# A two-layer attention and feed-forward trunk on one core: low parts of weight blocks moved from GpSimd to VectorE in the seven-product stage, and two tile pairs held instead of three

## Chip, cores and metric

One core of a Trainium2 chip runs the kernel. The metric is device time in microseconds, the median of several runs. The engines are named as the profile names them: PE (TensorE; PEld is its weight load), DVE (VectorE), ACT (ScalarE), POOL (GpSimd) and SP (SyncE, which here only issues DMAs).

## What is computed

Two transformer layers over 1024 latent tokens and 256 context tokens, width 1024. Layer 0 has windowed attention with grouped keys, layer 1 neighbourhood attention. Each layer ends with a gated feed-forward part, and that part is what the change touches:

```python
def swiglu(h, w_gu, w_down):
    gu = h @ w_gu
    return (jax.nn.silu(gu[..., :D_FF]) * gu[..., D_FF:]) @ w_down
...
        h = h + gt1 * y
        h = h + gt2 * swiglu(modulate(h, g_ffn[i], sh2, sc2), w_gate_up[i], w_down[i])
```

D_FF is 2816, which is 22 tiles of 128. Everything is float32.

## The kernel before

**Precision.** A float32 operand is split into a high part, rounded to the type that PE takes (fp32r), and a low part, the rest. A product is then three matmuls: high by high, high by low, low by high. `split` (L139) does this for a 128x512 block: ACT casts the high part (L141), and the engine given as `lo` subtracts it for the low part (L142).

**The stage.** `back` (L805) is the second half of a layer: output projection (`wo`, L860), normalisation, gate-up product, down product (L1061). In the gate-up product the contraction is cut into two halves of 512 and the 1024 tokens into two halves, and gate and up stand as the two block rows of a 2x2 block matrix a11, a12, a21, a22 (`load_gu`, L947: `raw` for gate blocks, `rawf` for up blocks, three buffers each). So a *tile pair* f (gate tile f and up tile f, f from 0 to 21) is a 2x2 by 2x2 block product, done with seven block products instead of eight. Each of them (`product`, L796) is 4 x 3 = 12 matmuls of 128x512, all recorded at L802. The token side is B11, B21, T1 to T4 and B22, made once per layer (`norm_lat`, `combine`). The weight side of a pair is a11, a12 and five sums (`weights`, L972): s1, s2, s3, a22 itself and a last s2. They are made on DVE by the helper `add` (L1159) into tiles `wt` and split into tiles `px`.

**Order of a pair.** `first` (L957) does the products with B11 and B21; ACT copies the first to u2 (L961) and puts the Silu of the sum into sg (L964). `second` (L967) adds the product with T2 to u2. `third` (L985) does T3 and T1 into two banks, which DVE reads as u3 (two additions); then it goes on filling the same two banks with T4 and B22, so those wait for u3. Of the results, s0 and y1 go to DRAM (L995, L1000). u2, sg and u3 are tiles `kp`, from eight buffers (`keep`, L818).

**What sets the order of the work.** The products with B11 and B21 of the first NPRE = 6 pairs are done ahead, while the other token blocks are made: their a11 and a12 are split into `wsp` tiles (`ew`, L1003 to L1006). Of these six pairs the u2 and sg of the first HELD = 3 stay in SBUF. Those of the rest are spilled to DRAM (L1019) and loaded back in the main loop (L1033). The instructions are put in order per engine by a scheduler when the program is built, so an edit of one place can move others. Each engine, and SP's DMA queue, then works strictly in its order.

Of the kernel before, what the change touches and what calls it, by code (L numbers as in the profile page):

```python
# [52 lines left out]
class Trunk:  # L53
# [751 lines left out]
    def back(self, layer, o):  # L805
# [8 lines left out]
        xslot = lambda dt=F32R: px.tile([P, 2, 512], dt, name="px", tag="px")  # L814
# [59 lines left out]
        def norm_lat(c):  # L874
            rs = self.rstd(st[c])
            if c == 0:
                self.preload(AF.Silu, rs[:, :1])
            yield
            pb = self.rows(rs, 4)
            yield  # L880
            g, sh = self.gsc[layer][1], mod[:, 3]
            for j in range(4):
                for k in (j, j + 4):
                    t, b = h[c, k], sh[:, k, 0:1]
                    nc.vector.scalar_tensor_tensor(out=t, in0=t, scalar=g[:, k, 0:1], in1=pb, op0=ALU.mult, op1=ALU.mult)
                    if c == 0:
                        nc.scalar.activation(out=t, in_=t, func=AF.Identity, bias=b)
                        B["B11" if k < 4 else "B21", j] = self.split(t, self.pslot(), alt(k + k // 4))
                        yield
            if c == 0:  # L890
                return
            for j in range(4):

                nc.vector.scalar_tensor_tensor(out=h[0, j], in0=h[1, j], scalar=sh[:, j, 0:1], in1=h[0, j],
                                               op0=ALU.add, op1=ALU.subtract)
                t2 = tmp()
                nc.vector.scalar_tensor_tensor(out=t2, in0=h[1, j + 4], scalar=sh[:, j + 4, 0:1], in1=h[0, j],
                                               op0=ALU.add, op1=ALU.subtract)
                B["t2", j] = t2
                B["T2", j] = self.split(t2, self.pslot(), "vector")  # L900
                for k in (j, j + 4):
                    nc.scalar.activation(out=h[1, k], in_=h[1, k], func=AF.Identity, bias=sh[:, k, 0:1])
                yield
# [43 lines left out]
        def load_gu(f, which):  # L947
            r = []
            for i, (y, half) in enumerate(which):
                t = (self.raw, rawf)[y]()  # L950
                nc.sync.dma_start(out=t, in_=a[f"w_gu{layer}"][f, y][:, half * 512:half * 512 + 512])
                r.append(t)
            return r
# [15 lines left out]
            self.product(pb, S, tb("T2"), True, True)  # L969
            self.add(u2, pb, u2, ALU.add)  # L970

        def weights(f, slot=xslot):  # L972

            a11, a12, a21, a22 = load_gu(f, ((0, 0), (0, 1), (1, 0), (1, 1)))
            if f >= NPRE:
                yield self.split(a11, xslot(), "gpsimd"), self.split(a12, xslot(), "gpsimd")
            s1 = self.add(wt(), a21, a22, ALU.add)
            s2 = sub(s1, a11)
            yield self.split(s2, xslot(), "gpsimd")
            s3 = sub(a11, a21)  # L980
            rest = [self.split(x, xslot(), "gpsimd") for x in (s3, s1, a22)]
            self.add(s2, a12, s2, ALU.subtract)
            yield rest + [self.split(s2, xslot(), "gpsimd")]

        def third(f, u2, sg, S):  # L985
            pd = self.bank()
# [12 lines left out]
            self.add(y1, y1, u3, ALU.mult)  # L999
            nc.sync.dma_start(out=self.ss[layer][f, :, 512:1024], in_=y1)  # L1000

        NPRE, HELD = 6, 3
        ew = []  # L1003
        for f in range(NPRE):
            a11, a12 = load_gu(f, ((0, 0), (0, 1)))
            ew.append([self.split(a11, self.slot(), "gpsimd"), self.split(a12, self.slot(), "vector")])  # L1006
        g1 = norm_lat(1)
        next(g1)
        if not last:
# [14 lines left out]
        for f in range(NF):  # L1024
            w = weights(f)
            if f >= NPRE:
                u = first(f, next(w))
            elif f < HELD:
                u = U[f]
            else:  # L1030
                u = keep(), keep()
                for i in range(2):
                    nc.sync.dma_start(out=u[i], in_=self.us[layer][f, i])  # L1033
            second(u[0], next(w))
            third(f, *u, next(w))
# [239 lines left out]
```

## Time and profile before

| what | value |
|---|---|
| median of 3 runs | 2933.78 us (2933.45 to 2938.89) |
| the profiled execution | 2932.86 us |
| its span | 2931.0 us |
| mean granted PE clock | 0.991 |
| PE busy | 97% |
| PEld busy | 79% |
| DVE busy | 54% |
| ACT busy | 38% |
| POOL busy | 37% |

The profile is one execution. Its span runs from the first to the last instruction, so it is 1.86 us shorter than that execution's time. Busy shares are averages over stages with different limits; a busy PE may still run at a lower clock.

### The profile page before, as it was taken

Reading aid. Unit: us, or ns where it says so; the run is one execution under the profiler, and the core shown is the slowest. Engines: PE = TensorE matmul, PEld = TensorE weight load, DVE = VectorE, ACT = ScalarE, POOL = GpSimd, SP = SyncE. Lnnn points to the kernel's source line nnn. Section 1 sums busy time; section 2 is a strip of 40 time slices with the busy share of each in tenths; the row PEclk is TensorE's granted clock in tenths of the full one; section 3 lists DMA queues with packets and bytes.
Section 4 is the critical chain, followed back from the end, with each engine's and each line's share of the span. In section 5 each row is a group of like instructions: output and inputs, shape, how many; then the busy total and the mean of one; then the engine's idle time right before and its main releaser. Section 6 shows DMA issues by size and latency. Waiting matters only on the chain.

```text
span 2931.0 us, 42778 instructions
## 1 busy us (share of the span) xinstructions
PE 2845.3 (97%) x15586; PEld 2305.4 (79%) x15586; DVE 1596.1 (54%) x2765; ACT 1124.5 (38%) x2263; POOL 1080.0 (37%) x1002
## 2 busy tenths in 40 slices
PE   6999999998999999999999999999999899999999
PEld 3667777787888887778998888777788788887887
DVE  5667777547655545446543344265656745555442
ACT  4323676434223232234543223265644422333120
POOL 3453242114555442233872345011102555554220
PEclk8999999999999999999999999999999999999999
DMA  7573342532322248544652554356653322226221
GB/s 265 189 232 94 101 126 80 165 110 100 129 83 80 81 165 287 193 159 136 191 184 88 151 153 139 99 159 162 179 171 124 125 93 82 87 83 205 87 90 61
DMA packets 305026, 402.09 MB, mean 137 GB/s; under 512 B 30000, under 2 KB 165680, under 8 KB 304816
## 3 DMA queue, kind: packets, MB, share of 16 engines
q1 hardware_dynamic: 235920, 360.81, 38.7%
q10 hardware_dynamic: 68896, 38.55, 4.5%
q8 instruction: 123, 2.02, 0.3%
q14 instruction: 87, 0.71, 0.1%
HBM read 316.69 MB, written 82.58 MB: 136 GB/s over the span
## 4 chain that ended last, share of the span: by engine, by line
PE 86%; DVE 4%; DMA 4%; ACT 2%; POOL 2%; issue 1%; SPq 1%; DVEq 0%; POOLq 0%; ACTq 0%
PE b L802 16%; PE bm L1061 16%; PE bm L802 10%; PE bm L352 10%; PE bm L860 7%; PE bm L1122 4%; PE b L352 3%; PE b L598 3%; PE b L588 3%; PE b L740 2%; PE b L1061 2%; PE b L725 2%; DMA qst<-q_s 2%; PE b L555 1%; PE b L159 1%
## 5 line engine op out<-in xcount | busy, mean ns | idle before, releaser
L1061 PE MATMUL bm<-pr,wsp 128*128 128x512 f32 x1920 | 440.3, 390 | 0.0
L1061 PEld LDWEIGHTS bm<-pr,wsp 128*128 128x128 f32 x1920 | 359.2, 188 | 82.1 <-issue 6.7
L802 PE MATMUL b<-wsp,px 128*128 128x512 f32 x1584 | 382.0, 395 | 11.0 <-DVE kp L1159 11.0
L802 PEld LDWEIGHTS b<-wsp,px 128*128 128x128 f32 x1584 | 300.9, 190 | 78.1 <-DVE kp L1159 11.9
L142 POOL TENSOR_TENSOR px<-wt,px 128x512 fp32r<-128x512 f32 x176 | 237.1, 1360 | 246.9 <-ACT px L141 238.9
L842 DVE SCALAR_TENSOR_TENSOR px<-bm,mod,px 128x512 f32<-128x512 f32 (+1 forms) x232 | 170.7, 739 | 279.8 <-PE bm L1061 223.5
L802 PE MATMUL bm<-pr,px 128*128 128x512 f32 x1296 | 317.3, 392 | 5.2 <-ACT kp L964 5.2
L141 ACT CAST wsp<-raw 128x512 fp32r<-128x512 f32 x306 | 188.2, 620 | 337.0 <-PE bm L1061 117.2
L142 POOL TENSOR_TENSOR wsp<-raw,wsp 128x512 fp32r<-128x512 f32 x144 | 191.7, 1339 | 299.6 <-ACT wsp L141 270.9
L802 PEld LDWEIGHTS bm<-pr,px 128*128 128x128 f32 x1296 | 243.4, 188 | 59.4 <-ACT kp L964 6.1
L352 PE MATMUL bm<-wsp,pr 128*128 128x512 f32 x1152 | 272.4, 393 | 0.0
L352 PEld LDWEIGHTS bm<-wsp,pr 128*128 128x128 f32 x1152 | 213.4, 188 | 43.4
L141 ACT CAST px<-wt 128x512 fp32r<-128x512 f32 x176 | 108.2, 622 | 347.1 <-PE b L802 312.7
L142 DVE TENSOR_TENSOR wsp<-raw,wsp 128x512 fp32r<-128x512 f32 x162 | 133.4, 829 | 138.7 <-ACT wsp L141 138.7
L860 PE MATMUL bm<-pr,wsp 128*128 128x512 f32 x768 | 176.8, 390 | 1.0 <-DVE ot L604 1.0
L860 PEld LDWEIGHTS bm<-pr,wsp 128*128 128x128 f32 x768 | 143.3, 188 | 30.6 <-DVE ot L604 1.2
L352 PE MATMUL b<-wsp,pr 128*128 128x512 f32 x576 | 149.3, 413 | 18.4 <-ACT pr L261 6.6
L292 POOL TENSOR_TENSOR hrs<-hss,mhalf 128x8 f32<-128x8 f32 (+1 forms) x66 | 104.7, 1587 | 167.3 <-DVE hss L290 162.4
L705 DVE CUSTOM_DVE_ANT_0 pr<-b,wsp,big 128x640 f32<-128x640 f32 (+1 forms) x128 | 107.4, 846 | 88.1 <-PE b L700 87.1
L352 PEld LDWEIGHTS b<-wsp,pr 128*128 128x128 f32 x576 | 110.3, 197 | 56.2 <-issue 12.0
L1159 DVE TENSOR_TENSOR t<-b,kp 128x512 f32<-128x512 f32 x88 | 60.3, 685 | 144.3 <-PE b L802 144.3
L1122 PE MATMUL bm<-prc,wsp 128*128 128x256 f32 x1056 | 133.6, 285 | 0.0
(203 smaller groups left out, 4917.1 us busy)
## 6 DMA issues: line engine op xcount, KB each, us to landing
raw<-w_gu SPq DMA_DIRECT2D x156, 256.0 KB, 2.7
qst<-q_s SPq DMA_DIRECT2D x288, 128.0 KB, 3.1
rawf<-w_gu SPq DMA_DIRECT2D x132, 256.0 KB, 3.0
raw<-w_down SPq DMA_DIRECT2D x110, 256.0 KB, 3.3
wsp<-w_ada SPq DMA_DIRECT2D x48, 512.0 KB, 7.1
pr<-w_ada SPq DMA_DIRECT2D x48, 512.0 KB, 6.5
s_s<-t SPq DMA_DIRECT2D x88, 256.0 KB, 2.0
rawf<-s_s SPq DMA_DIRECT2D x88, 256.0 KB, 3.1
```

The costliest lines, as they stand in the source:

```text
L141: self.nc.scalar.copy(out=w[:, 0, :n], in_=x)
L142: getattr(self.nc, lo).tensor_tensor(out=w[:, 1, :n], in0=x, in1=f32(w[:, 0, :n]), op=ALU.subtract)
L292: nc.gpsimd.tensor_tensor(out=rs[:, :nh], in0=ss[:, :nh], in1=self.mhalf[:, :nh], op=ALU.pow)
L352: self.nc.tensor.matmul(ps, x, y, start=(k == 0 and i == 0), stop=(k == KT - 1 and i == 2))
L588: nc.tensor.transpose(tp[:, h * P:(h + 1) * P], u["p"][h][:, i * P:(i + 1) * P], self.ident)
L598: nc.tensor.matmul(op[64 * r:64 * r + 64, :256], u["v"][:, kt, :], u["pt"][i][:, 256 * r:256 * r + 256], start=(i == 0), stop=(i == len(kt ...
L705: nc.vector.tensor_tensor_reduce(out=pt[:, :nl + 256], in0=V, in1=u["bias"][x][m // 7][:, b0:b0 + nl + 256], scale=-1.0, scalar=self.big, ...
L802: self.nc.tensor.matmul(ps, x, y, start=first and k == 0 and i == 0, stop=last and k == 3 and i == 2, skip_group_check=True)
L842: nc.vector.scalar_tensor_tensor(out=h[c, k], in0=ps, scalar=mod[:, ty, k, z:z + 1], in1=h[c, k], op0=ALU.mult, op1=ALU.add)
L860: nc.tensor.matmul(ps[:, :n], x, y, start=(k == 0 and i == 0), stop=(k == KT - 1 and i == 2))
L1061: nc.tensor.matmul(ps, x, y, start=(z == 0 and i == 0), stop=(z == len(parts) - 1 and i == 2))
L1122: nc.tensor.matmul(ps[:, q * CTX:(q + 1) * CTX], x, y, start=(k == 0 and i == 0), stop=(k == KT - 1 and i == 2))
```

## The change

Three things change. For the six early pairs all low parts of weight blocks are taken on DVE: a11 in `ew` (a12 was there already) and the five splits of `weights`. For the other 16 pairs four of seven low parts are on DVE (a11, a12, the first s2, s3) and three stay on POOL (s1, a22, the last s2). HELD becomes 2. An unused argument goes, and one line is added, so lines from L976 on are one higher in the changed kernel.

```diff
-        def weights(f, slot=xslot):
+        def weights(f):
 
             a11, a12, a21, a22 = load_gu(f, ((0, 0), (0, 1), (1, 0), (1, 1)))
+            late = "vector" if f < NPRE else "gpsimd"
             if f >= NPRE:
-                yield self.split(a11, xslot(), "gpsimd"), self.split(a12, xslot(), "gpsimd")
+                yield self.split(a11, xslot(), "vector"), self.split(a12, xslot(), "vector")
             s1 = self.add(wt(), a21, a22, ALU.add)
             s2 = sub(s1, a11)
-            yield self.split(s2, xslot(), "gpsimd")
+            yield self.split(s2, xslot(), "vector")
             s3 = sub(a11, a21)
-            rest = [self.split(x, xslot(), "gpsimd") for x in (s3, s1, a22)]
+            rest = [self.split(x, xslot(), lo) for x, lo in ((s3, "vector"), (s1, late), (a22, late))]
             self.add(s2, a12, s2, ALU.subtract)
-            yield rest + [self.split(s2, xslot(), "gpsimd")]
+            yield rest + [self.split(s2, xslot(), late)]
...
-        NPRE, HELD = 6, 3
+        NPRE, HELD = 6, 2
         ew = []
         for f in range(NPRE):
             a11, a12 = load_gu(f, ((0, 0), (0, 1)))
-            ew.append([self.split(a11, self.slot(), "gpsimd"), self.split(a12, self.slot(), "vector")])
+            ew.append([self.split(a11, self.slot(), "vector"), self.split(a12, self.slot(), "vector")])
```

The scheduler turns this into new orders. On DVE, layer 0, from the u2 of pair 0 (`kp_7205<-bm_7488`) to its u3 (`kp_7530<-b1_7517`, the first of two), before. `px` and `wsp` rows are low parts (`wsp_7467` one of the token side), `wt` rows make weight sums of the pairs 1 (`wt_7589`), 2 (`wt_7693`, `wt_7695`, `wt_7714`) and 3 (`wt_7803`); numbers only tell tiles apart.

```order
L1159 TENSOR_TENSOR kp_7205<-bm_7488,kp_7205 128x512 [waits PE_49]
L1159 TENSOR_TENSOR wt_7693<-rawf_7689,rawf_7691 128x512 [waits DMAHW4_49,DMAHW0_49,Pool_49]
L1159 TENSOR_TENSOR wt_7589<-raw_7581,wt_7589 128x512 [waits Pool_49]
L1159 TENSOR_TENSOR wt_7695<-wt_7693,raw_7685 128x512 [waits DMAHW6_49,DVE_49,Pool_49]
L142 TENSOR_TENSOR wsp_7467<-px_6486,wsp_7467 128x512 [waits PE_49,Activation_49]
L1159 TENSOR_TENSOR wt_7714<-raw_7685,rawf_7689 128x512 [waits Pool_49]
L1159 TENSOR_TENSOR wt_7695<-raw_7687,wt_7695 128x512 [waits DMAHW7_49,Pool_49]
L1159 TENSOR_TENSOR wt_7803<-rawf_7799,rawf_7801 128x512 [waits DMAHW2_49,DMAHW1_49]
L1159 TENSOR_TENSOR kp_7530<-b1_7517,kp_7205 128x512 [waits DMAHW6_49,DMAHW3_49,PE_49]
```

The same place in the changed kernel, again from the u2 of pair 0 to its u3; two low parts (`px_7512`, `px_7516`) stand just ahead of it.

```order
L1160 TENSOR_TENSOR kp_7205<-bm_7490,kp_7205 128x512 [waits PE_49]
L142 TENSOR_TENSOR px_7593<-wt_7591,px_7593 128x512 [waits Activation_49]
L142 TENSOR_TENSOR px_7612<-wt_7610,px_7612 128x512 [waits Activation_49]
L142 TENSOR_TENSOR px_7615<-wt_7589,px_7615 128x512 [waits Activation_49]
L142 TENSOR_TENSOR px_7618<-rawf_7587,px_7618 128x512 [waits Activation_49]
L142 TENSOR_TENSOR wsp_7469<-px_6486,wsp_7469 128x512 [waits PE_49,Activation_49]
L1160 TENSOR_TENSOR wt_7591<-raw_7583,wt_7591 128x512 [waits DMAHW4_49,DVE_49]
L1160 TENSOR_TENSOR wt_7699<-rawf_7695,rawf_7697 128x512 [waits DMAHW0_49]
L1160 TENSOR_TENSOR wt_7701<-wt_7699,raw_7691 128x512 [waits DMAHW6_49,DVE_49]
L1160 TENSOR_TENSOR wt_7720<-raw_7691,rawf_7695 128x512
L142 TENSOR_TENSOR px_7622<-wt_7591,px_7622 128x512 [waits Activation_49]
L1160 TENSOR_TENSOR kp_7532<-b1_7519,kp_7205 128x512 [waits DMAHW5_49,DMAHW1_49,PE_49]
```

Five low parts of pair 1 have come in ahead of u3, the `wt` of pair 3 has gone behind it, and the waits for POOL are gone.

On SP's queue, layer 0, from the first spill on, before (`u0_s` rows are spills; the numbers of `kp` rise with the pair).

```order
L1019 DMA u0_s_105<-kp_7292 128x512 [waits DMAHW1_49,Activation_49]
L1019 DMA u0_s_105<-kp_7306 128x512 [waits Activation_49]
L1019 DMA u0_s_105<-kp_7323 128x512 [waits Activation_49]
L951 DMA rawf_7691<-w_gu0 128x512 [waits DMAHW4_49,Pool_49]
L1019 DMA u0_s_105<-kp_7337 128x512 [waits DMAHW5_49,Activation_49]
L1019 DMA u0_s_105<-kp_7354 128x512 [waits DMAHW6_49,Activation_49]
L951 DMA raw_7795<-w_gu0 128x512 [waits DMAHW7_49,DVE_49]
L951 DMA raw_7797<-w_gu0 128x512 [waits DMAHW0_49,DVE_49]
L951 DMA rawf_7799<-w_gu0 128x512 [waits DMAHW1_49]
L951 DMA rawf_7801<-w_gu0 128x512 [waits DMAHW2_49,Pool_49]
```

And in the changed kernel, from the first spill on:

```order
L1020 DMA u0_s_105<-kp_7263 128x512 [waits Activation_49]
L1020 DMA u0_s_105<-kp_7277 128x512 [waits DMAHW2_49,Activation_49]
L1020 DMA u0_s_105<-kp_7294 128x512 [waits Activation_49]
L1020 DMA u0_s_105<-kp_7308 128x512 [waits DMAHW4_49,Activation_49]
L1020 DMA u0_s_105<-kp_7325 128x512 [waits DMAHW5_49,Activation_49]
L1020 DMA u0_s_105<-kp_7339 128x512 [waits DMAHW6_49,Activation_49]
L1020 DMA u0_s_105<-kp_7356 128x512 [waits DMAHW7_49,Activation_49]
L951 DMA rawf_7697<-w_gu0 128x512 [waits DMAHW0_49,DVE_49]
L951 DMA rawf_7805<-w_gu0 128x512 [waits DMAHW1_49,DVE_49]
L951 DMA raw_7801<-w_gu0 128x512 [waits DMAHW2_49,DVE_49]
```

Seven spills now stand ahead of the next `rawf`, which waits for DVE instead of POOL. PE's order is the same but for the early pairs of each layer, where the second product of pair 5 comes ahead of three remainders of ten matmuls. On ACT only the Silu of pair 5 moves, ahead of three casts.

## Rows read from the trace of the kernel before

**Rows 1.** The page, part 1: busy time, share of the span, instructions.

```profile
PE 2845.3 (97%) x15586; PEld 2305.4 (79%) x15586; DVE 1596.1 (54%) x2765; ACT 1124.5 (38%) x2263; POOL 1080.0 (37%) x1002
```

**Rows 2.** Waits of PE: line waited for what: us in total, times, longest.

```profile
PE b L802 <- DVE kp L1159: 11.0, 2, 5.6
...
PE bm L802 <- ACT kp L964: 5.2, 2, 2.6
```

**Rows 3.** Busy time by engine, 760 to 1080 us; last: PE clock, DMA share, GB/s.

```profile
core 0: us, PE busy (x) PEld busy (x) DVE busy (x) ACT busy (x) POOL busy (x), PEclk, DMA share, GB/s
760.00:1080.00 320.00, 320.00 (x1400) 262.56 (x1399) 167.85 (x183) 94.22 (x163) 160.76 (x116) 1.00 0.26 88
```

**Rows 4.** Timeline of PE, layer 0: start, us, instruction; idle time before in brackets.

```profile
691.03 0.80 PE L802 MATMUL bm<-pr,px 128*128 128x512 f32 x1 [2.62 <-ACT kp L964]
...
695.49 2.22 PE L802 MATMUL bm<-pr,px 128*128 128x512 f32 x9
...
707.60 1.87 PE L802 MATMUL bm<-pr,px 128*128 128x512 f32 x7
...
715.02 2.46 PE L802 MATMUL b<-wsp,px 128*128 128x512 f32 x10
723.10 13.58 PE L802 MATMUL b<-wsp,px 128*128 128x512 f32 x48 [5.62 <-DVE kp L1159]
736.52 2.91 PE L802 MATMUL bm<-pr,px 128*128 128x512 f32 x12
```

**Rows 5.** Timeline of PE, the same place of layer 1.

```profile
2274.24 0.71 PE L802 MATMUL bm<-pr,px 128*128 128x512 f32 x1 [2.61 <-ACT kp L964]
...
2278.99 2.22 PE L802 MATMUL bm<-pr,px 128*128 128x512 f32 x9
...
2298.41 2.46 PE L802 MATMUL b<-wsp,px 128*128 128x512 f32 x10
2306.28 13.87 PE L802 MATMUL b<-wsp,px 128*128 128x512 f32 x48 [5.42 <-DVE kp L1159]
2319.99 2.91 PE L802 MATMUL bm<-pr,px 128*128 128x512 f32 x12
```

**Rows 6.** Busy time by engine just after the second wait (columns as in rows 3).

```profile
723.10:728.00 4.90, 4.90 (x12) 3.84 (x13) 4.74 (x8) 1.24 (x2) 1.82 (x2) 0.50 0.20 63
```

**Rows 7.** Timeline of all engines, 700 to 723 us, layer 0.

```profile
700.49 4.51 POOL L142 TENSOR_TENSOR px<-rawf,px 128x512 fp32r<-128x512 f32 x1 [25.91 <-ACT px L141]
...
703.74 0.70 DVE L1159 TENSOR_TENSOR kp<-bm,kp 128x512 f32<-128x512 f32 x1
...
704.45 0.58 ACT L961 COPY kp<-bm 128x512 f32<-128x512 f32 x1
...
705.03 0.33 SPq L951 DMA_DIRECT2D rawf<-w_gu  x1
...
710.95 1.78 DVE L1159 TENSOR_TENSOR wt<-wt,raw 128x512 f32<-128x512 f32 x1
...
716.55 0.90 SPq L951 DMA_DIRECT2D rawf<-w_gu  x2
...
721.75 0.69 DVE L1159 TENSOR_TENSOR wt<-rawf 128x512 f32<-128x512 f32 x1 [5.01 <-DMA rawf<-w_gu]
722.36 0.68 DVE L1159 TENSOR_TENSOR kp<-b,kp 128x512 f32<-128x512 f32 x1
```

**Rows 8.** Timeline of DVE, just before: five low parts back to back.

```profile
697.72 3.10 DVE L142 TENSOR_TENSOR wsp<-px,wsp 128x512 fp32r<-128x512 f32 x5
```

**Rows 9.** DMA issues: count, KB each, median us to landing.

```profile
rawf<-w_gu SPq DMA_DIRECT2D x132, 256.0 KB, 3.0
...
kp<-u_s SPq DMA_DIRECT2D x12, 256.0 KB, 3.2
```

**Rows 10.** Groups of DVE instructions by form, 760 to 1080 us: busy, mean ns | idle.

```profile
L1159 DVE TENSOR_TENSOR wt<-wt,raw 128x512 f32<-128x512 f32 x15 | 25.4, 1696 | 15.8 <-POOL px L142 15.8
```

**Rows 11.** Tile `wt`: idle of DVE before it, until: us, times.

```profile
  DMA rawf<-w_gu: 115.3, 35
```

## Prediction

> **What bounds the kernel now.** I read the shares of the page first: TensorE (PE) is busy for 97% of the span [rows 1]. Only time in which PE stands still, or runs at its lower clock, can be won. The waits of PE come next, longest first [rows 2]. In the changed stage (its matmuls are L802) there are two kinds: 11.0 us in 2 waits for `kp` from VectorE (DVE, the helper at L1159), and 5.2 us in 2 for `kp` from ScalarE (ACT, L964). PE never waits there for the low part of a weight block, the thing that the change moves. One stretch by itself [rows 3] shows how full the rest is: 1400 matmuls in 320.00 us, all of it busy, at clock 1.00. That is my unit: 320.00 / 1400 = 0.2286 us per matmul. GpSimd (POOL) is busy half of that stretch, DVE 52%, and neither holds anything up.
>
> The places of the waits come from PE's timeline, layer 0 [rows 4] and layer 1 [rows 5]; they are copies of each other. The *second wait* of layer 0: ten matmuls start at 715.02, so the next could start at 717.31 (10 x 0.2286); it starts at 723.10, 5.8 us late. After that stretch without work the granted clock is 0.50 for 4.9 us [rows 6], the lower of its two levels (1.2 and 2.4 GHz): the 48 matmuls from 723.10 to 736.52 take 13.42 us instead of 10.97, 2.45 us more. In layer 1 the same sums are 2306.28 - 2300.70 = 5.6 and 13.71 - 10.97 = 2.7. **Second wait with its clock: 8.2 + 8.3, 16.6 us** before rounding. The *first wait* (idle 2.62 us, then 13 matmuls in 4.46 us instead of 2.97) costs 4.1 us in layer 0, and 2.61 + 1.77 = 4.4 in layer 1: 8.5 in all.
>
> Why the second wait is there stands in the timeline of all engines [rows 7]. PE had left a bank at 707.60 that it can go on filling only once DVE has read it: this is u3 of tile pair 0, the `kp<-b,kp` at 722.36. DVE works in order, and u3 stood behind subtractions of weight blocks. The first of them needed a `rawf` block whose load left SP only at 705.03, since its buffer was still read by a POOL subtraction of 4.51 us (700.49 to 705.0). The next ones took 1.78 us beside POOL, as at 710.95; u3 itself took 0.68. The last before u3 waited 5.01 us for another pair of `rawf` loads, which SP issued at 716.55, behind loads whose buffers those slow operations held.
>
> **The change, part by part.**
> *Low parts of pairs 0 to 5 on DVE.* Per layer 6 (a11) + 30 leave POOL, which then has none of this stage's subtractions to do until pair 6. DVE's order has u3 eleven rows after the u2 of pair 0 (eight before), but behind the first `wt` of pair 2 alone, no longer that of pair 3. I walk that queue with the pitch of DVE rows that run back to back alone, 3.10 / 5 = 0.62 us with the end of the last [rows 8], so 0.61. DVE reaches the first added row at 703.74, where u2 started before; the rows ahead of it are as they were. Two low parts, u2, four low parts, a T part and one `wt` are nine rows: 709.2. The load of `rawf` leaves SP once its reader, the first added row, is done (704.4) and behind the spill of what ACT copied until 705.03: at 705.5. It lands after 3.0 us, the page's median [rows 9], before 709.2. Three `wt` and one low part put u3 at 711.7, done at 712.4. PE has meanwhile, from 707.6, one whole product (pair 5's second, now ahead) and three remainders of 10: 42 x 0.2286 = 9.6, so it wants u3 at 717.2. Slack 4.8 us. The same walk gives 715.4 against 720.4 for the second u3 of pair 0, and 718.4 against 723.6 for the first of pair 1. With a landing of 5 us, as long as the wait before 721.75, the slack is 3.6. So the second wait goes, and the low clock behind it: -16.6 us.
>
> *Four of seven on DVE afterwards.* 64 more per layer make 100, 200 in the run: 200 x 0.61 to 0.69 = 122 to 138 us of DVE, beside PE. A pair then has 15 DVE operations (11 before) in 84 x 0.2286 = 19.2 us; 15 x 0.69 = 10.4 alone. What POOL adds is the question. In the stretch of rows 3, DVE's 183 operations take 167.85 us, where 183 x 0.61 = 111.6; POOL runs 116 there, so 56.2 / 116 = 0.48 us per POOL operation. Three remain per pair: 10.4 + 1.5 = 11.9 us of 19.2. The other bound takes 1.70, the dearest group [rows 10], for each of the ten operations that read two SBUF tiles: 10 x 1.70 + 5 x 0.69 = 20.4, more than 19.2. I take 11.9, since an operation takes 1.78 only while POOL runs, and POOL's part shrinks. The Trainium skill ("SBUF — State Buffer", Who interferes with whom) says that a VectorE instruction with two SBUF inputs and a GpSimd one that reads SBUF lock each other out of a shared port for a whole instruction. That rule charges a delay to each meeting with a POOL operation, so the sum by it stays at -16.6; by the other bound it would be +22. The trace agrees with a lock (the 1.78 and the 0.68 above).
>
> *In pairs 0 to 5* a pair has 16 DVE operations, 11.0 us, in 60 x 0.2286 = 13.7. DVE also waits for `rawf`, 115.3 us in 35 waits [rows 11], 3.3 each: 14.3, 0.6 over. I charge nothing, since the low parts run about two pairs ahead (eleven `px` slots, five per pair); without that cover it is 0.6 x 4 pairs x 2 layers = 5 us, kept for the range.
>
> *Two held instead of three.* Per layer two spills and two reloads of 256 KB more; a reload lands in 3.2 us [rows 9], at a DMA share of 0.26 in the stage, and an issue takes SP 0.33 [rows 7]. SP's order has seven spills in one row ahead of the next `rawf`, already in the walk above. The reload of pair 2 can leave by about 714 and is wanted after 729. u3's buffer was last emptied by the fifth of those spills, whose copy is older than 704.45. Zero.
>
> *First wait.* Here ACT works in order: the Silu that frees the bank stands behind casts that follow DVE's normalisation. Both engines' orders are the same there: 0.
>
> Sum: -16.6 us. The profiled execution (2932.86, span 2931.0) becomes 2916.3; the median shown is 0.9 above it, so **2917.2**. What follows the stage is bound by PE as well, so the gain carries to the end.
>
> **Rivals.**
> *Only one half comes* (one layer, or a landing later than 8.6 us, from where slack turns into wait): -8 us, 2925. For it: one late load is enough. Against: 3.6 to 5 us of slack at three places.
> *The wait only moves*: 2933.8. DVE is still in order, and u3 still stands behind a `wt` that waits for a load. It costs as much as before if that load lands 14 us after its issue; the longest wait here is 5.0.
> *More goes*: the first wait too, as POOL no longer meets DVE ahead of it: 16.6 + 8.5 = 25.1, 2909. Against: the rows there are the same.
> *DVE becomes the bound in pairs 6 to 21*: if each of ten operations per pair meets POOL, 20.4 - 19.2 = 1.2 us x 16 pairs x 2 layers = 38, less 16.6: +22, 2956. It decides from 19.2 us of DVE per pair. For it: the 1.70 of the dearest group. Against: three POOL operations can hardly meet ten.
>
> **How the numbers follow.** Forecast 0.68 (2912 to 2922: 5 us for pairs 0 to 5 above, as much for part of the first wait below), one half 0.10, only moves 0.10, more goes 0.05, DVE the bound 0.07. A measurement of this kernel tells about 0.2% (6 us) from no change. Faster: 0.68 + 0.10 + 0.05 = 0.83; same 0.10; slower 0.07. The range takes in the forecast, the half and part of "more": 2909 to 2927.
>
> **What would show it.** Right: of PE's waits the 11.0 us for `kp` from DVE are gone and the 5.2 us for ACT stay; PE is busy at clock 1.00 from 717 to 737 and at its twin in layer 1; POOL has 200 instructions less; DVE operations in pairs 0 to 5 take 0.69. Wrong: a new wait of PE for `px` from DVE, or more than 19 us of DVE per pair after pair 6.

## The result, and the profile after

The changed kernel takes **2920.35 us** (median of 4 runs, 2916.41 to 2922.67). The kernel before, on the same chip, takes 2935.53 us (4 runs, the three above and one more). The ratio is **0.9946**, 95% interval 0.9929 to 0.9963: faster by 0.4 to 0.7%, some 15 us. The profiled execution took 2916.41 us (span 2914.6) where that of before took 2932.86, so 16.45 us less.

The first thing to read is the waits of PE, which answer to [rows 2]:

```profile
PE bm L802 <- ACT kp L964: 5.2, 2, 2.6
PE bm L802 <- DVE pr L142: 0.2, 1, 0.2
```

The 11.0 us of `kp` from DVE are gone, the 5.2 us of ScalarE are unchanged. The timeline of PE in layer 0 shows both places (columns as in [rows 4]):

```profile
690.78 0.50 PE L802 MATMUL bm<-pr,px 128*128 128x512 f32 x1 [2.61 <-ACT kp L964]
691.25 3.02 PE L802 MATMUL bm<-pr,wsp 128*128 128x512 f32 x12
694.10 1.55 PE L802 MATMUL bm<-pr,px 128*128 128x512 f32 x6
...
711.84 2.45 PE L802 MATMUL b<-pr,px 128*128 128x512 f32 x10
714.13 5.20 PE L802 MATMUL b<-wsp,px 128*128 128x512 f32 x22
719.16 0.62 PE L802 MATMUL bm<-pr,px 128*128 128x512 f32 x2
```

The row of 22 at 714.13 is the place of the second wait: ten matmuls of a remainder and, with no bracket between, the twelve that need u3. At 0.2286 us each PE asked for u3 at 714.13 + 2.29 = 716.4. What VectorE did meanwhile stands in the timeline of all engines, which answers to [rows 7]:

```profile
703.51 0.68 DVE L142 TENSOR_TENSOR px<-rawf,px 128x512 fp32r<-128x512 f32 x1
...
704.62 3.54 SPq L951 DMA_DIRECT2D rawf<-w_gu  x2
...
708.93 0.68 DVE L1160 TENSOR_TENSOR wt<-rawf 128x512 f32<-128x512 f32 x1
...
711.46 0.68 DVE L1160 TENSOR_TENSOR kp<-b,kp 128x512 f32<-128x512 f32 x1
```

The low part at 703.51 takes 0.68 us on DVE (4.51 on POOL before), its raw block is free, SP issues the next load at 704.62, the `wt` that needs it runs at 708.93, and u3 is done at 712.14, 4.3 us before PE asks. Before, u3 started at 722.36. The first load itself leaves only 0.4 us earlier than before (705.03 there). What is new is that the rows behind it take some 0.6 us each instead of up to 1.78, and that the sum which stood 5.01 us for the loads of 716.55 now comes behind u3.

The windows answer to [rows 3, 6]: the place of the second wait in each layer, then 300 us of the late pairs. The last three numbers are PE clock, DMA share and GB/s.

```profile
core 0: us, PE busy (x) PEld busy (x) DVE busy (x) ACT busy (x) POOL busy (x), PEclk, DMA share, GB/s
717.00:737.00 20.00, 20.00 (x89) 16.40 (x88) 19.76 (x33) 7.26 (x12) 0.00 (x0) 1.00 0.60 197
2290.00:2310.00 20.00, 20.00 (x90) 16.39 (x89) 19.98 (x35) 6.48 (x11) 0.00 (x0) 1.00 0.64 203
700.00:760.00 60.00, 60.00 (x264) 49.27 (x263) 53.48 (x87) 21.55 (x38) 0.00 (x0) 1.00 0.49 163
760.00:1060.00 300.00, 300.00 (x1313) 246.14 (x1312) 175.19 (x235) 88.75 (x154) 65.11 (x47) 1.00 0.25 85
```

PE is busy all through and at clock 1.00. DVE is now busy nearly all of 717 to 737 (19.76 of 20 us), so what it does there no longer has room to be slow. On the page [rows 1] POOL goes from 1002 to 802 instructions:

```profile
PE 2840.7 (97%) x15586; PEld 2303.1 (79%) x15586; DVE 1642.0 (56%) x2965; ACT 1123.9 (39%) x2263; POOL 790.9 (27%) x802
```

### The profile page after: what moved, and what is told of

The parts are those of the page before. It is cut to its first block, busy times and chain, and to the rows that moved or that the text cites. A ratio compares the mean times of both kernels' runs of the same rounds, so it can differ in the third digit from the quotient of the medians.

```text
span 2914.6 us, 42716 instructions
## 1 busy us (share of the span) xinstructions
PE 2840.7 (97%) x15586; PEld 2303.1 (79%) x15586; DVE 1642.0 (56%) x2965; ACT 1123.9 (39%) x2263; POOL 790.9 (27%) x802
## 4 chain that ended last, share of the span: by engine, by line
PE 86%; DVE 3%; DMA 2%; issue 1%; POOL 1%; ACT 1%; SPq 0%; DVEq 0%; ACTq 0%; POOLq 0%
PE b L802 16%; PE bm L1062 16%; PE bm L802 11%; PE bm L352 11%; PE bm L860 7%; PE bm L1123 4%; PE b L598 3%; PE b L588 3%; PE b L740 2%; PE b L1062 2%; PE b L725 2%; PE b L352 2%; DMA qst<-q_s 1%; PE b L555 1%; PE b L697 1%; PE b L700 1%
## 5 line engine op out<-in xcount | busy, mean ns | idle before, releaser
L142 POOL TENSOR_TENSOR px<-wt,px 128x512 fp32r<-128x512 f32 x64 | 91.3, 1427 | 626.6 <-ACT px L141 383.4
L142 POOL TENSOR_TENSOR wsp<-raw,wsp 128x512 fp32r<-128x512 f32 x132 | 174.9, 1333 | 249.0 <-ACT wsp L141 224.5
L142 DVE TENSOR_TENSOR wsp<-raw,wsp 128x512 fp32r<-128x512 f32 x174 | 140.4, 812 | 145.7 <-ACT wsp L141 145.5
```

What stands on the lines that cost most here:

```text
L142: getattr(self.nc, lo).tensor_tensor(out=w[:, 1, :n], in0=x, in1=f32(w[:, 0, :n]), op=ALU.subtract)
```

## The experiments

Each kernel was timed in five rounds against the kernel before on the same chip. The runs of the table are from two chips, so they are compared with each other by their ratios. A ratio is taken over the runs and is not exactly the quotient of the two medians. "Wait" is the idle time of PE for `kp` from VectorE in both layers, from its profile.

| run | what it is | median, us | before, us | ratio (95%) | wait, us |
|---|---|---|---|---|---|
| e1_held2 | before, two pairs held | 2937.42 | 2937.44 | 1.0000 (0.9990 to 1.0010) | 11.9 |
| e4_late_dve | before, late pairs moved | 2935.56 | 2937.44 | 0.9999 (0.9986 to 1.0012) | 10.9 |
| e3_early_dve | before, early pairs moved | 2920.84 | 2937.44 | 0.9946 (0.9932 to 0.9960) | none |
| e10_order_alone | before, u3 ahead in order | 2933.08 | 2936.25 | 0.9988 (0.9978 to 0.9998) | 7.0 |
| e5_a22_two_pairs | before, 4 low parts moved | 2929.39 | 2937.44 | 0.9975 (0.9964 to 0.9986) | 5.6 |
| e11_a22_six_pairs | before, 12 low parts moved | 2923.66 | 2936.25 | 0.9953 (0.9937 to 0.9968) | 3.6 |
| e17_pool_beside | e3 with POOL kept busy | 2944.39 | 2935.66 | 1.0026 (1.0015 to 1.0036) | 17.7 |
| e6_all_on_vector | after, 7 of 7 on DVE | 2921.16 | 2936.25 | 0.9948 (0.9931 to 0.9965) | none |
| after_again | after | 2920.73 | 2935.66 | 0.9941 (0.9924 to 0.9958) | none |
| e14_t1_behind_t2 | after, T1 later | 2917.46 | 2936.25 | 0.9931 (0.9916 to 0.9946) | none |
| e14_again | the same | 2916.46 | 2935.66 | 0.9928 (0.9914 to 0.9943) | none |
| e16_silu_first | after, T1 and biases later | 2923.73 | 2935.66 | 0.9958 (0.9941 to 0.9974) | none |

### Which part of the change brings the gain

**Two held instead of three, alone.**

```diff
-        NPRE, HELD = 6, 3
+        NPRE, HELD = 6, 2
```

> The kernel before with one number changed: two tile pairs held instead of three; every low part stays on GpSimd. My theory (pair 0's u3 comes late because it stands on VectorE behind work that waits for a raw buffer which GpSimd still reads) gives the time of the kernel before: the second wait stays in both layers (idle 5.8 and 5.6 us of TensorE for kp from VectorE), within 2 us of the kernel before. The rival that the smaller hold brings the gain expects no such wait and some 15 us less than before.

Measured: no difference, and the wait is all there (11.9 us). The smaller hold neither costs nor brings anything by itself.

**Four of seven in the late pairs, alone.**

```diff
+            lo = "gpsimd" if f < NPRE else "vector"
-                yield self.split(a11, xslot(), "gpsimd"), self.split(a12, xslot(), "gpsimd")
+                yield self.split(a11, xslot(), lo), self.split(a12, xslot(), lo)
-            yield self.split(s2, xslot(), "gpsimd")
+            yield self.split(s2, xslot(), lo)
-            rest = [self.split(x, xslot(), "gpsimd") for x in (s3, s1, a22)]
+            rest = [self.split(x, xslot(), z) for x, z in ((s3, lo), (s1, "gpsimd"), (a22, "gpsimd"))]
```

> The kernel before with four of seven low parts on VectorE in pairs 6 to 21 alone; pairs 0 to 5 are as before and three pairs stay held. My theory: no gain, within 2 us of the kernel before, the second wait of 5 to 6 us in each layer still there, and VectorE in pairs 6 to 21 busy for about 11 us of each pair's 19 us without a wait of TensorE on it. The rival that the late pairs bring the gain expects some 15 us less; the rival that VectorE becomes the bound there expects some 20 us more.

Measured: no difference. The 128 instructions that move here are worth nothing, and cost nothing. VectorE is busy for 182.18 us of the 300 from 760 on (158.66 before), 11.7 of a pair's 19.2, with POOL still at work beside it (66.03 us).

**The low parts of pairs 0 to 5, alone.**

```diff
+            lo = "vector" if f < NPRE else "gpsimd"
-            yield self.split(s2, xslot(), "gpsimd")
+            yield self.split(s2, xslot(), lo)
...
-            ew.append([self.split(a11, self.slot(), "gpsimd"), self.split(a12, self.slot(), "vector")])
+            ew.append([self.split(a11, self.slot(), "vector"), self.split(a12, self.slot(), "vector")])
```

> The kernel before with the low parts of tile pairs 0 to 5 alone on VectorE; three pairs stay held, and pairs 6 to 21 keep all low parts on GpSimd. My theory: the whole gain, 15 to 17 us less than before, no wait of TensorE for kp from VectorE in either layer, and the first wait (some 2.6 us for the Silu on ScalarE) still there. The rival that the four of seven in the late pairs bring it (fewer GpSimd operations beside VectorE for the whole stage) expects no gain here.

Measured: the whole gain, 0.9946, the ratio of the full change. These 72 instructions are the change; the other two parts could be left out.

### Why it does: order, buffers, or speed

**Order alone.** Pair 3's first sum, which waits for a raw block, is issued behind u3 of pair 0. All low parts stay on POOL.

```diff
-            s1 = self.add(wt(), a21, a22, ALU.add)
+            with ExitStack() as order:
+                if f == 3:
+                    order.enter_context(tc.issue_after(getattr(u3s[0], "ins", u3s[0])))
+                s1 = self.add(wt(), a21, a22, ALU.add)
...
-            u3 = self.add(keep(), pd, u2, ALU.add)
+            u3 = keep()
+            u3s[f] = nc.vector.tensor_tensor(out=u3, in0=pd, in1=u2, op=ALU.add)
```

> The kernel before with every low part where it was, on GpSimd; only the order of VectorE is changed: in each layer the first sum of tile pair 3 (the one that waits for its raw blocks) is issued after u3 of pair 0. If u3 was late only because it stood behind that sum, VectorE is free for it at about 716.7 us, TensorE asks for it at 717.3, and the second wait with its low clock goes at this place (up to 16.6 us less than before). If the raw blocks held by slow GpSimd operations are the cause, the wait comes back at the next sum that TensorE needs from VectorE, as in the run with one low part of two pairs moved (3.0 us of idle time some 25 us later): about 6 to 9 us less than before.

Measured: 3 us won of 16, less than the 6 to 9 that the second branch expected. The timeline of this kernel, all engines, shows where the wait went:

```profile
717.85 0.90 SPq L951 DMA_DIRECT2D rawf<-w_gu  x2
717.96 0.68 DVE L992 TENSOR_TENSOR kp<-b,kp 128x512 f32<-128x512 f32 x1
...
722.37 1.42 DVE L1163 TENSOR_TENSOR wt<-rawf 128x512 f32<-128x512 f32 x1 [3.73 <-DMA rawf<-w_gu]
723.71 0.68 DVE L1163 TENSOR_TENSOR kp<-bm,kp 128x512 f32<-128x512 f32 x1
724.31 0.68 DVE L1163 TENSOR_TENSOR kp<-b,kp 128x512 f32<-128x512 f32 x1
...
725.04 10.09 PE L802 MATMUL b<-wsp,px 128*128 128x512 f32 x36 [3.32 <-DVE kp L1163]
```

u3 (now L992) runs at 717.96, in time. Right behind it DVE stands still for 3.73 us at the same `wt`, whose load again left SP only at 717.85, and now the next sum is late (724.31), so PE waits 3.32 us for that. Here the new order moved the late load's wait and did not take it away.

**One low part of two pairs.** The low part of a22 is the last reader of its raw block.

```diff
-            rest = [self.split(x, xslot(), "gpsimd") for x in (s3, s1, a22)]
+            rest = [self.split(x, xslot(), "vector" if x is a22 and f < 2 else "gpsimd") for x in (s3, s1, a22)]
```

> The kernel before with one low part (that of a22) of tile pairs 0 and 1 alone on VectorE, four operations in the whole program. My theory: in VectorE's order u3 of pair 0 then stands ahead of the piece of pair 3 that waits for its raw buffer, so most of the gain comes already: 10 to 16 us less than before and the second wait gone or under 2 us. The rival that GpSimd's load on the shared path slows VectorE throughout (so that all 42 early low parts must go) expects under 5 us of gain and a second wait of 3 us or more.

Measured: 7 us, less than the 10 to 16 that I expected and more than the rival's 5: neither branch. (The expectation's 42 per layer counts the low parts of a12 too, which are on VectorE in the kernel before; 36 are to move. This profile's execution was the longest of its twelve, so only places and idle times are read from it.) Its timeline of PE:

```profile
720.01 11.58 PE L802 MATMUL b<-wsp,px 128*128 128x512 f32 x48
...
745.16 8.58 PE L802 MATMUL b<-wsp,px 128*128 128x512 f32 x24 [3.03 <-DVE kp L1159]
```

At the old place there is no wait left; a new one comes 25 us later, for the u3 of a later pair.

**The same for six pairs** (the condition `f < NPRE` in the line above).

> As the run with the a22 low part of pairs 0 and 1 on VectorE, but for all of pairs 0 to 5: 12 operations in the whole program leave GpSimd, the other 72 of those pairs stay. That run had a new wait of 3.0 and 2.5 us for u3 of a later pair. If GpSimd's holding of the raw block of a22 delays the loads in that pair too, this wait goes and the time is that of the whole change: 14 to 17 us less than before. If it is GpSimd's slowing of VectorE in general (1.78 us operations beside it), the wait stays and the time is 6 to 9 us less than before.

Measured: 2923.66, some 13 us less than before: between the two branches. With 12 of the 72 early instructions moved (the expectation miscounted: 60 stay), most of the gain is there. The profile shows waits that are left, in PE's timeline of layer 0 and 1 and in that of DVE ahead of the first:

```profile
742.41 7.37 PE L802 MATMUL b<-wsp,px 128*128 128x512 f32 x24 [1.82 <-DVE kp L1159]
...
2321.32 5.78 PE L802 MATMUL b<-wsp,px 128*128 128x512 f32 x24 [1.75 <-DVE kp L1159]
```

```profile
735.66 0.69 DVE L1159 TENSOR_TENSOR wt<-rawf 128x512 f32<-128x512 f32 x1 [1.71 <-DMA rawf<-w_gu]
...
738.22 2.99 POOL L142 TENSOR_TENSOR px<-wt,px 128x512 fp32r<-128x512 f32 x2 [3.11 <-ACT px L141]
738.26 1.80 DVE L1159 TENSOR_TENSOR wt<-raw,wt 128x512 f32<-128x512 f32 x1
...
740.59 1.17 DVE L1159 TENSOR_TENSOR wt<-wt,raw 128x512 f32<-128x512 f32 x1
741.68 0.68 DVE L1159 TENSOR_TENSOR kp<-b,kp 128x512 f32<-128x512 f32 x1
```

Ahead of the late sum at 741.68 stand two `wt` operations that took 1.80 and 1.17 us beside POOL instead of 0.68. That is 1.6 us more, nearly the 1.82 that PE waits. But VectorE had also stood 1.71 us for a load, until 735.66, so this wait is not shown to be POOL's slowing alone.

**POOL busy, but holding no raw block.** From the kernel e3_early_dve, with a POOL subtraction added after each low part of these pairs:

```diff
+        scr = fp.tile([P, 512], mybir.dt.bfloat16, name="scr", tag="scr", bufs=1)
...
+            def split(x):
+                w = self.split(x, xslot(), lo)
+                if f < NPRE:
+                    nc.gpsimd.tensor_tensor(out=scr, in0=f32(w[:, 0]), in1=f32(w[:, 1]), op=ALU.subtract)
+                return w
```

> As the run with the low parts of pairs 0 to 5 alone on VectorE, but GpSimd does a subtraction of the same size after each of the 30 that belong to pairs 0 to 5 in each layer (not the a11 of the first stage), from the finished px tile into a scratch tile that nobody reads. So GpSimd runs beside VectorE as it did before, and holds no raw block and no wt tile. VectorE's order is that of the run without the extra work. If the held buffers made u3 late, the time is within 4 us of that run and no wait of TensorE for kp from VectorE is over 1 us. If GpSimd's slowing of VectorE made it late, waits of 3 us or more come back in each layer and the time is 8 us or more above that run.

Measured: 2944.39 us, 24 more than e3_early_dve (0.8% by the ratios) and 0.26% slower than the kernel before. The branch that I had not believed came true in time. Its timeline (all engines), and its window, columns as above:

```profile
708.14 10.14 POOL L981 TENSOR_TENSOR scr<-px 128x512 bf16<-128x512 f32 x6 [29.47 <-DVE px L142]
...
708.51 0.68 DVE L1167 TENSOR_TENSOR kp<-bm,kp 128x512 f32<-128x512 f32 x1
...
709.12 4.60 DVE L142 TENSOR_TENSOR px<-wt,px 128x512 fp32r<-128x512 f32 x3
...
713.64 1.78 DVE L142 TENSOR_TENSOR px<-rawf,px 128x512 fp32r<-128x512 f32 x1
...
721.28 0.68 DVE L1167 TENSOR_TENSOR kp<-b,kp 128x512 f32<-128x512 f32 x1
```

```profile
700.00:760.00 60.00, 50.12 (x208) 39.59 (x207) 59.97 (x71) 19.39 (x36) 31.37 (x21) 0.94 0.35 113
```

Beside the six POOL operations, DVE operations that read two SBUF tiles take 1.78 us (and 4.60 for three, where three alone take 1.9), while `kp<-bm,kp`, which reads one operand from PSUM, takes 0.68 in the middle of them. DVE is busy for 59.97 of 60 us with 71 instructions; the changed kernel has 87 done in 53.48. The wait for pair 0's u3 is only 1.05 us here (5.62 before), and those that cost are later, 2.46 and 5.30 us (2.47 and 3.56 in layer 1), when the delays have added up. The Trainium skill ("SBUF — State Buffer", Who interferes with whom) says that a VectorE instruction with two SBUF inputs contends with a GpSimd one that reads SBUF, for a port pair that is an exclusive lock, and that one with at most one SBUF input, outside the two-port modes, does not. The rows agree (1.78 against 0.68 us).

So two things can make a sum late: a raw block that POOL still reads, so that the next load comes late, and POOL's slowing of VectorE. In the kernel before both lie on one path to the second wait. This is the chain of work that ended in it, in order of time (start, us, what):

```profile
700.49 4.53 POOL px L142
...
705.03 3.13 DMA rawf<-w_gu
...
710.95 1.78 DVE wt L1159
712.73 1.71 DVE wsp L142
714.43 1.72 DVE wt L1159
...
716.17 0.33 SPq L951
...
717.07 4.59 DMA rawf<-w_gu
```

POOL's read of a raw block holds the first load until 705.03 (the changed kernel, where VectorE reads that block, sends it at 704.62, so at this load the hold is worth 0.4 us). Slow rows of VectorE follow, and the last of them holds a `raw` load (716.17) that stands on SP's queue ahead of the load for pair 3. In e11, where VectorE reads the block of a22, the loads come earlier (all engines):

```profile
705.90 1.19 DVE L142 TENSOR_TENSOR px<-rawf,px 128x512 fp32r<-128x512 f32 x1
...
706.56 0.90 SPq L951 DMA_DIRECT2D rawf<-w_gu  x2
```

Two `rawf` loads have left by 707.46, where the kernel before sent one at 705.03 and the next two at 716.55 [rows 7].

What the runs give is this. Order alone is worth 3 us (e10), the twelve low parts of a22 some 13 us (e11), all 72 some 16 us (e3). The intervals of e11 and e3 overlap, so the last step is not clear of noise in the time; it shows as the 3.6 us of waits that e11 keeps and e3 does not. That slow rows make the sums late with no raw block held by POOL is shown by e17, though there VectorE also carries the low parts. What stays open is the share of each in the wait of the kernel before: e11 frees the block, but it also changes VectorE's order (u3 starts at 718.06 there, ahead of the sum of pair 3) and takes 12 slowing operations from POOL.

### DVE as the bound in the late pairs

```diff
-            late = "vector" if f < NPRE else "gpsimd"
+            late = "vector"
```

> The changed kernel with all seven low parts on VectorE in pairs 6 to 21 as well; GpSimd has nothing to do there. My theory: 18 VectorE operations per pair, none slowed by GpSimd any more, so 0.69 us each, 12.4 us of a pair's 19.2: the time of the changed kernel within 3 us, and no wait of TensorE for px from VectorE. The rival that VectorE becomes the bound in these pairs expects over 20 us more.

Measured: 2921.16, as the changed kernel, and no wait for `px` from DVE. The window of 300 us:

```profile
760.00:1060.00 300.00, 300.00 (x1313) 246.14 (x1312) 184.40 (x283) 89.39 (x155) 0.00 (x0) 1.00 0.26 85
```

48 more DVE instructions than after need only 9.2 us more, since POOL is silent: 184.40 / 283 = 0.65 us each.

### The wait that stayed

**The changed kernel once more**, as a base for the last runs.

> The changed kernel once more, on the chip of the next three runs and as their base: 14 to 17 us less than the kernel before, by either theory.

Measured: 2920.73, 0.9941.

**T1 behind T2.** `self.two` are the two instructions of the last split.

```diff
                 B["T2", j] = self.split(t2, self.pslot(), "vector")
+                B["two"] = self.two
...
-                B["T1", j] = self.split(h[0, j], self.slot(), "vector")
+                with ExitStack() as order:
+                    for x in B["two"]:
+                        order.enter_context(tc.issue_after(getattr(x, "ins", x)))
+                    B["T1", j] = self.split(h[0, j], self.slot(), "vector")
```

> The changed kernel with the split of T1 (a cast on ScalarE and a subtraction on VectorE, four times per layer) issued behind that of T2. The first wait of the stage is for a Silu on ScalarE which stands behind casts, four of them T1's; without those the Silu can run as soon as TensorE has filled its bank (688.2 us instead of 690.15). My theory: the 2.6 us waits for kp from ScalarE shrink to under 1 us in both layers, and 4 to 8 us less than the changed kernel are seen, its low clock included. The rival: the wait only moves, since TensorE next asks for the low parts of T2, which come from a VectorE that is as busy; then under 2 us are won and the wait is named pr from VectorE.

> T1 behind T2 once more, on the chip of the changed kernel's second run: the waits for kp from ScalarE were 1.9 us each instead of 2.6, so 1.5 us of idle time and what the low clock after it costs, 2 to 5 us less than the changed kernel. The rival that only the chips differed expects the changed kernel's time within 1 us.

Measured: 2917.46 and 2916.46, 3 to 4 us under the changed kernel's 2920.73. The intervals of the ratios overlap (0.9914 to 0.9943 against 0.9924 to 0.9958 on the same chip), so the difference from the changed kernel is likely and not settled; from the kernel before it is 0.5 to 0.9%. The wait did not go under 1 us as I expected:

```profile
688.25 0.60 ACT L141 CAST pr<-t 128x512 fp32r<-128x512 f32 x1
688.75 0.72 ACT L903 ACTIVATE px<-px,mod 128x512 f32<-128x512 f32 x1
689.38 0.57 ACT L968 ACTIVATE kp<-bm 128x512 f32<-128x512 f32 x1
...
690.00 1.83 PE L802 MATMUL bm<-pr,px 128*128 128x512 f32 x4 [1.86 <-ACT kp L968]
```

T1's casts are gone from ahead of the Silu, but a cast of T2 and a bias operation have moved up into their place.

**Silu first.** Half of the bias operations are issued behind the Silu too.

```diff
                 for k in (j, j + 4):
-                    nc.scalar.activation(out=h[1, k], in_=h[1, k], func=AF.Identity, bias=sh[:, k, 0:1])
+                    with ExitStack() as order:
+                        if k >= 4:
+                            order.enter_context(tc.issue_after(getattr(sgs[2], "ins", sgs[2])))
+                        nc.scalar.activation(out=h[1, k], in_=h[1, k], func=AF.Identity, bias=sh[:, k, 0:1])
```

> As T1 behind T2, and four of the eight bias operations of ScalarE (the second half of h) issued behind the Silu of pair 2 as well. ScalarE then comes to that Silu at about 687.6 us, before TensorE has filled the bank (688.1), so the first wait is some 0.6 us instead of 1.9. My theory: 2 to 6 us less than T1 behind T2, as the low clock after the wait may go too. The rival: the bias operations that now come later delay VectorE's T2 and T3 rows, and TensorE waits for pr from VectorE instead; no gain or a loss of 1 to 3 us.

Measured: 2923.73, 7 us more than T1 behind T2. PE's timeline:

```profile
694.15 0.49 PE L802 MATMUL bm<-pr,px 128*128 128x512 f32 x1 [0.69 <-ACT kp L971]
...
703.23 4.52 PE L802 MATMUL bm<-pr,wsp 128*128 128x512 f32 x12 [2.59 <-ACT kp L968]
```

The first wait shrank to 0.69 us, as worked out. But the scheduler put the next twelve matmuls with `wsp` ahead of thirteen others, where they need a bank before ScalarE has copied it: 2.59 us, and the low clock behind it (those twelve take 4.38 us at a granted clock of 0.63). The rival was right that nothing is won, but its loss of 1 to 3 us was too small and its engine the wrong one.

## Why the prediction was right

*The second wait, 16.6 us.* The step held in both layers: PE no longer waits for VectorE, and its clock is 1.00 at both places. The medians differ by 15.2 us, and the measured median is 3.2 us above the forecast of 2917.2; 1.75 us of that is the median of before, which is 2935.53 here and was 2933.78 in the sum. The two profiled executions differ by 16.45 us. That this is so close to 16.6 is partly luck: each is a single execution, and in layer 0 of the changed one the low clock after the first wait did not come (1.1 us, last section), which the prediction had not counted.

*The walk of VectorE's queue.* The load of `rawf` was put at 705.5 and left at 704.62; u3 at 711.7 and ran at 711.46. PE asked at 716.4, not 717.2, since it began its 42 matmuls some 0.8 us earlier (716.4 less 9.6 is 706.8, not 707.6). So the slack was 4.3 us instead of 4.8. The walk came this close because VectorE alone is regular: the eleven rows from u2 (704.72) to u3 (711.46) are 0.61 us apart.

*The cause.* The prediction named both the held raw block and the 1.78 us operations, without shares. The runs show that both count and do not part them: the twelve low parts of a22 bring some 13 us (e11), by an earlier load, a new order and a little less slowing at once.

*Four of seven afterwards, zero.* Right (e4). In the changed kernel the 11.9 us of DVE per pair are 175.19 / 300 x 19.2 = 11.2. My price per POOL operation was 0.48 us; with the same pitch of 0.61 it is (175.19 - 235 x 0.61) / 47 = 0.68, with the 184.40 / 283 of e6 it is 0.47. The pitch, not the price, was the loose end.

*Pairs 0 to 5, zero.* Right: PE stands nowhere, though DVE is full there (19.76 of 20 us). The 3.3 us of waiting for `rawf` per pair that the prediction weighed did not come there: from 700 to 760 us VectorE waits 3.5 us for it in six such sums (10.7 in five before). How thin the cover is shows in e17: with slow rows VectorE is full, PE waits 17.7 us for it, and the kernel becomes slower than before.

*Two held, zero.* Right (e1).

*First wait stays.* Right: 5.2 us before and after. The low clock behind it is another matter (last section).

*The rivals.* "Only one half comes" did not happen: both layers lost the wait. Nor did "more goes": the 5.2 us for ScalarE are still there. "The wait only moves" did not happen to the full change, but it is what the partial ones did: e10, e5 and e11 each moved the wait to a later sum. "DVE becomes the bound in pairs 6 to 21" failed even with all seven low parts there (e6). In pairs 0 to 5, where VectorE has less room, it came true once POOL was kept busy beside it (e17).

## What to carry to other kernels

When a wait ends on an in-order engine, walk back along that engine's queue to the load that it stood for, and from there to the reader that held the buffer. Try that reader first: here 12 instructions of 72 gave most of what there was. Reordering the waiting engine alone won 3 us here and handed the rest of the wait to a later sum.

Before moving work from GpSimd to VectorE, look at how full VectorE is in that stretch. In pairs 6 to 21, with room to spare, the move cost nothing although GpSimd worked on beside it (e4). In pairs 0 to 5, where VectorE is nearly full, it paid when GpSimd fell silent (e3), since VectorE's slow rows went with it; with both busy it was worse than no move (e17).

## What was not expected of the hardware

The same wait does not always bring the low clock. In the changed kernel the first wait is 2.61 us in each layer. In layer 0 the twelve matmuls after its first start at 691.25 and the next at 694.10: 2.85 us, nearly the 2.74 of 12 x 0.2286. In layer 1 they take 4.38:

```profile
2266.25 0.50 PE L802 MATMUL bm<-pr,px 128*128 128x512 f32 x1 [2.61 <-ACT kp L964]
2266.72 4.54 PE L802 MATMUL bm<-pr,wsp 128*128 128x512 f32 x12
2271.10 2.22 PE L802 MATMUL bm<-pr,px 128*128 128x512 f32 x9
```

The windows of these 13 matmuls (columns as above) show the granted clock in layers 0 and 1. In the kernel before, layer 0 has 4.46 us at 0.67.

```profile
690.78:694.10 3.32, 3.32 (x13) 2.54 (x14) 3.32 (x7) 3.32 (x7) 0.00 (x0) 1.00 0.41 158
2266.25:2271.10 4.85, 4.85 (x14) 3.69 (x14) 4.85 (x9) 4.85 (x10) 0.00 (x0) 0.65 0.28 108
```

This is not the work of the change: e1_held2, whose low parts are all where they were, has 3.37 us at clock 1.00 in layer 0, and the changed kernel's second profile has the low clock in both layers. In e11_a22_six_pairs the two waits of 1.82 and 1.75 us are followed by 24 matmuls in 7.37 and in 5.78 us (rows above). So the 4.1 and 4.4 us that the prediction read off for the first wait are 2.6 us of idle time, in every profile here that keeps this order, and some 0.4 to 1.9 us more in the 13 matmuls behind it, as the low clock comes or not; in a sum, such a wait is a range.
